# A hybrid mLSTM / RWKV-7 / S5 step: other places for the in-projections computed ahead, and a last stage whose sums are on VectorE

## The chip, the cores and the metric

The kernel runs on one core of a Trainium2 chip. The metric is device time in microseconds. A core has TensorE (PE in the profile; its weight loads stand apart as PEld), VectorE (DVE), ScalarE (ACT), GpSimd (POOL) and SyncE (SP). Each engine works off its own instructions in order. SP computes nothing here: every transfer of this kernel is issued from its one queue, in order.

## What is computed

One layer runs over 520 tokens: 512 of one prompt and 8 samples with states of their own. The width is 1024.

```
x   = LayerNorm(x)
z   = x @ W_in                       # 12424 columns, cut among the parts below
y_A = (mLSTM(xm, ig, fg) gated by og, normed, + skip) * silu(z_A) @ w_bm
y_B = (RWKV-7(r, k, v, decay, a) normed, + bonus)     * silu(z_B) @ w_br
y_C = (S5(u) + D u, GELU, GLU)                        * silu(z_C) @ w_bs
x'  = LayerNorm(ALPHA * x + (sum_b sigmoid(g_b) * y_b) @ w_out)
```

The new states of all three mixers are outputs too. Everything is f32, and so are the weights that are read.

## The kernel before

**In-projections.** The normed input stands transposed in SBUF, cut in two parts `xh` and `xl`. An in-projection of 128 columns (`inproj`, line 142) loads 128 columns of `W_in` in two halves through the three `wraw` buffers (`load_w`, lines 123 to 132). ScalarE copies each half to `whi` (line 130), VectorE subtracts to get `wlo` (line 131); both tiles have two buffers. Then 48 matmuls (`gemm`, line 134) compute hi*hi + hi*lo + lo*hi over eight row tiles, for 256 and for 264 tokens. An output product (`w_br`, `w_bs`, `w_bm`) has the same form with other left and right sides.

**Fills.** In-projections that are needed later are computed ahead, one at a time, and parked in DRAM. They are 44 items of the list `fills` (lines 303 to 316): eight of S5's input u (`fill_u`), then 36 more (`fill_z`), in the order og, z_C, z_A, the gate of branch S5 (eight each), xm (two) and the gate of branch RWKV (two). Each takes a turn of the weight buffers and ends with a store (`zsave` or `ud`). Their pool `fl` stands on the left side and is closed after RWKV (line 362).

**RWKV** (`rwkv`, from line 393) needs 25 in-projections of its own: the small ranks first, then for each of eight column tiles k, r and v. `rcol` (line 421) runs one fill ahead of each. A projection ends with the small copy `shn` on GpSimd (line 354). The column tiles go in four pairs. A pair has its elementwise work, an inverse (62 dependent VectorE operations, lines 595 to 601), and a serial recurrence of eight steps (`chain`, line 633), in which TensorE, ScalarE and VectorE hand over to each other; each step has one copy `rs` on VectorE (line 652). After the last pair the 19 fills that remain are written down in one go (line 796).

**S5, mLSTM and the merge.** S5 (line 945) is interleaved with branch RWKV of the merge, `other(1)`; mLSTM (line 1235) with branch S5 of the merge, which begins with the GLU. `other(0)`, the branch of mLSTM, comes by itself. `out_branch` (line 1562) multiplies by the branch's output matrix, one column tile after another; VectorE gates the result, and for the second and third branch GpSimd adds it to the sum `mg` (line 1588).

**Last stage.** `final` (line 1642) splits `mg`, loads and splits `w_out`, and makes the closing matmuls. The residual needs the input norm's gain and offset: GpSimd multiplies and adds them on five tiles of 1024 columns (line 1682). The saved input `xr` (2 MB) goes into the space of `xh`, and the broadcast rows `xg` into that of `xl`, so that their loads stand behind the last in-projection. The rows `lng` of the last norm go into the space of the gates.

**What sets the order.** The program order is a priority. A planner (Tile, with a simulated timeline) lays each engine's instructions in an order of its own: an instruction goes ahead when its inputs and buffers are there by its reckoning, and what comes first in the program has precedence. So fills that are written down last run between the instructions of the last pair. `issue_after(x)` keeps the instructions of a block that are on the engine of x behind x.

Of the kernel before, what the change touches and what calls it, by code (L numbers as in the profile page):

```python
# [15 lines left out]
P = 128  # L16
D = 1024
# [16 lines left out]

C_XM, C_IG, C_FG, C_OG, C_ZM = 0, 1024, 1028, 1032, 2056
C_RC, C_ZR, C_U, C_ZS, C_GM = 3080, 6280, 7304, 8328, 9352


@with_exitstack
def hybrid_step(ctx: ExitStack, tc: tile.TileContext, I, O):  # L40
# [79 lines left out]
    RB = 3  # L120
    ahead = {}

    def load_w(src, m=P):
        hi = wp.tile([P, KT, P], F32R, tag="whi", bufs=2, name="whi")
        lo = wp.tile([P, KT, P], F32R, tag="wlo", bufs=2, name="wlo")
        src = src.rearrange("(k p) c -> p k c", p=P)
        for k, eng in ((slice(0, KT // 2), weng[0]), (slice(KT // 2, KT), weng[1])):
            raw = wp.tile([P, KT // 2, P], F32, tag="wraw", bufs=RB, name="wraw")
            dma(raw[:, :, 0:m], src[:, k])
            A.activation(hi[:, k, 0:m], raw[:, :, 0:m], AF.Copy)  # L130
            eng.tensor_tensor(lo[:, k, 0:m], raw[:, :, 0:m], hi[:, k, 0:m].bitcast(F32), op=ALU.subtract)  # L131
        return hi, lo
# [135 lines left out]
    flc = ExitStack()  # L268
    fl = flc.enter_context(tc.tile_pool(name="fl", bufs=1))
    zsave, fills = {}, []  # L270

# [31 lines left out]
    for ct in range(KT):  # L303
        fills.append((fill_u, ct))
    for b, c0 in enumerate((C_OG, C_ZS, C_ZM, C_GM + 2 * D)):
        zd = dr.tile([KT, P, N], F32, name=f"zsave{b}")
        for ct in range(KT):
            fills.append((fill_z, (c0 + ct * P, zd[ct])))

    zx = dr.tile([KT, P, N], F32, name="zsave5")  # L310
    for ct in range(2):
        fills.append((fill_z, (C_XM + ct * P, zx[ct])))

    zd = dr.tile([KT, P, N], F32, name="zsave4")
    for ct in range(2):
        fills.append((fill_z, (C_GM + D + ct * P, zd[ct])))

# [43 lines left out]
    rwkv(tc, I, O, env)  # L361
    flc.close()
    mrg = Merge(tc, I, O, env)
    weng[:] = [V, V]
    mrg.open("mr", 1, 4)
    interleave(s5(tc, I, O, env), mrg.other(1), 1.5)
    mrg.pctx.close()
    weng[:] = [V, V]
    mrg.open("ms", 1, 4)
    interleave(mlstm(tc, I, O, env), mrg.s5(), 0.42)  # L370
    mrg.pctx.close()
    mrg.open("mf", 3, 5)
    for _ in mrg.other(0, ahead=True):
# [19 lines left out]
def rwkv(tc, I, O, env):  # L393
# [24 lines left out]
    def rt(name, tag="t", bufs=TB):  # L418
        return rp.tile([P, N], F32, tag=tag, bufs=bufs, name=name)

    def rcol(j):
        rc = rp.tile([P, 1 + N], F32, tag="rc", bufs=1, name="rc")
        e.fill()
        return e.rcol(j, rc, rt("xr"))
# [370 lines left out]
    dma(e.ybsave[:, :, T:N].rearrange("c p b -> p c b"), bvs)  # L795
    e.fill(len(e.fills))
    ctx2.close()
# [147 lines left out]
def s5(tc, I, O, env):  # L945
# [20 lines left out]
    for pi in range(KT // 2):  # L966
# [48 lines left out]
        for j in range(2):  # L1015
# [23 lines left out]
            for h in range(2):  # L1039
                tr(p[:, h * P:(h + 1) * P], kt[:, h])  # L1040
            for h in range(2):
                A.activation(ko[:, j].rearrange("p (m h c) -> p m h c", h=2, c=SC)[:, :, h],
                             p[:, h * P:(h + 1) * P].rearrange("p (m h c) -> p m h c", h=2, c=SC)[:, :, h], AF.Copy)
            gms.append(gm)
            ebs.append(eb)
        kf = ko.rearrange("p j c -> p (j c)")
        V.tensor_tensor(kf[0:SC], kf[0:SC], dm.rearrange("p g c -> p (g c)"), op=ALU.add)
# [461 lines left out]
class Merge:  # L1509
# [52 lines left out]
    def out_branch(self, b, wname, ah, al, permuted=False, gates=None):  # L1562
        e, V, G = self.e, self.tc.nc.vector, self.tc.nc.gpsimd
        mg = self.mg
        for ct in range(KT):
            if gates:
                th = gates[ct]
            else:
                th = self.gate(b, ct, self.t2("gth"))
                yield  # L1570
            hi, lo = e.load_w(self.I[wname][0, :, ct * P:(ct + 1) * P])

            def ev(s, n, p):
# [9 lines left out]
                for dst, g, y in parts:  # L1583
                    if self.first:
                        V.scalar_tensor_tensor(dst, g, 1.0, y, op0=ALU.add, op1=ALU.mult)  # L1585
                    else:
                        V.scalar_tensor_tensor(g, g, 1.0, y, op0=ALU.add, op1=ALU.mult)
                        G.tensor_tensor(dst, dst, g, op=ALU.add)
            e.gemm(hi, lo, ah, al, ev)
# [52 lines left out]
    def final(self):  # L1642

        e, I, O, fp, mg = self.e, self.I, self.O, self.fp, self.mg
        V = self.tc.nc.vector
        dma, split = e.dma, e.split
        mh, ml_ = self.pair("mg")
        for ct in range(KT):
# [3 lines left out]
        lng = fp.tile([P, 2, D], F32, tag="gt", bufs=1, name="lng")  # L1652
        xr = e.xtp.tile([P, 4, D], F32, tag="xh", name="xr")
        xg = e.xtp.tile([P, 3, D], F32, tag="xl", name="xg")
        G = self.tc.nc.gpsimd
        dma(xr, e.xsave[0:T].rearrange("(a p) c -> p a c", p=P))
        dma(xg[0:NB, 2], e.xsave[T:N])
        for j, nm in enumerate(("ln_in_g", "ln_in_b")):
            dma(xg[:, j], I[nm].unsqueeze(0).to_broadcast([P, D]))
        dma(lng[:, 0, :], I["ln_g"].to_broadcast([P, D]))  # L1660
        dma(lng[:, 1, :], I["ln_b"].to_broadcast([P, D]))
        ws = []
# [11 lines left out]
        for hf in range(2):  # L1674
            woh, wol = ws[hf]
            for tt in (4, 0, 1, 2, 3) if hf else (0, 4, 1, 2, 3):
                n = P if tt < 4 else NB
                x = xr[:, tt] if tt < 4 else xg[:, 2]
                if hf == 0:
                    sts[tt] = fp.tile([P, 2, 6], F32, tag="fst", bufs=5, name="fst")  # L1680
                    for j, op in enumerate((ALU.mult, ALU.add)):
                        G.tensor_tensor(x[:n], x[:n], xg[:n, j], op=op)
                p = e.psg.tile([P, 512], F32, tag="g", name="g")
# [60 lines left out]
```

## Time and profile before

| | |
|---|---|
| runs | 1379.88, 1379.0, 1373.04 us; median 1379.0 |
| profiled execution | 1378.35 us |
| its span, first to last instruction | 1376.3 us |
| TensorE busy | 1254.4 us, 91% |
| VectorE busy | 959.2 us, 70% |
| ScalarE busy | 679.5 us, 49% |
| GpSimd busy | 242.8 us, 18% |
| granted clock of TensorE, mean | 0.947 |

The times of the profile are microseconds from the span's start, except where a row says ns. In rows of the profile `L62` is line 62 of the kernel; a tile written and the tiles read stand as out<-in, and `x48` is a count. A busy TensorE is not one at its peak: its matmuls overlap, and the duration shown for one is longer than the time from its start to the next one's. The granted clock is a share of full speed. In the chain of waits each piece is work, or a transfer, on which the next piece waited.

The stages are: entry to about 60 us; the RWKV loop with its 25 projections to 526 us; its exit with the last pair to about 722; S5 with branch RWKV to about 930; mLSTM with branch S5 to about 1250; branch mLSTM and the closing stage to the end.

### The profile page before, as it was taken

To read this page: it belongs to the slowest core of one execution; us is meant where nothing else is said; L and a number is where in the kernel's file an instruction comes from. 1 tells how busy PE (TensorE), PEld (TensorE's weight loads), DVE (VectorE), ACT (ScalarE), POOL (GpSimd) and SP (SyncE) were. 2 spreads that over 40 slices of the span, in tenths; PEclk is the share of its full clock that TensorE was granted. 3 is DMA by queue.
4 is the path that set the end of the run, shared out by engine and by line. 5 is a ranking of instruction groups with operands and counts; after the bars stand their busy time and mean duration, and the time that the engine had idled before them with its cause. 6 is when DMAs were issued, how large, how long until landed. Compare 5 with 4: busy or idle time off the path is not lost.

```text
span 1376.3 us, 27658 instructions
## 1 busy us (share of the span) xinstructions
PE 1254.4 (91%) x10509; PEld 1147.4 (83%) x10509; DVE 959.2 (70%) x2157; ACT 679.5 (49%) x1492; POOL 242.8 (18%) x396
## 2 busy tenths in 40 slices
PE   4969999999998999999985988996999999999887
PEld 4969988889897889999865988996989888899855
DVE  6694594569357834768836998995776775555857
ACT  4547657465746674453222332334765774453220
POOL 1402211123122311105200020000000011104600
PEclk8989999999999999999977999997999999999999
DMA  6333332213121312354518444546676866465331
GB/s 185 95 91 109 91 97 64 74 50 87 52 78 46 89 55 85 96 147 141 160 29 149 110 97 104 130 99 179 208 225 207 275 200 203 138 201 189 92 107 62
DMA packets 246707, 168.49 MB, mean 122 GB/s; under 512 B 54808, under 2 KB 222106, under 8 KB 246302
## 3 DMA queue, kind: packets, MB, share of 16 engines
q1 hardware_dynamic: 246574, 166.72, 43.0%
q8 instruction: 83, 1.36, 0.4%
q14 instruction: 50, 0.41, 0.1%
HBM read 125.18 MB, written 39.20 MB: 119 GB/s over the span
## 4 chain that ended last, share of the span: by engine, by line
PE 35%; DVE 7%; DMA 5%; issue 2%; SPq 2%; ACT 1%; POOL 0%; DVEq 0%; ACTq 0%; POOLq 0%
PE g L62 23%; PE qk L62 2%; PE ys L62 2%; DVE wlo L131 2%; SPq L53 2%; PE s L62 1%; DMA wraw<-in_w_bm_dram 1%; PE nd L62 1%; PE pn L62 1%; PE v L62 1%; DMA cn<-in_state_mlstm_c_dram 1%; PE cn L62 1%; DMA wraw<-in_w_out_dram 1%; DMA br<-in_s_b_im_dram 1%; PE cy L62 1%
## 5 line engine op out<-in xcount | busy, mean ns | idle before, releaser
L62 PE MATMUL g<-xh,whi 128*128 128x264 f32 (+1 forms) x1552 | 461.2, 297 | 37.8 <-DVE th L1541 16.0
L62 PE MATMUL g<-xl,whi 128*128 128x264 f32 (+1 forms) x1552 | 457.1, 295 | 2.1 <-DVE xl L217 2.1
L62 PE MATMUL g<-xh,wlo 128*128 128x264 f32 (+1 forms) x1552 | 454.8, 293 | 0.2 <-DVE wlo L131 0.2
L62 PEld LDWEIGHTS g<-xh,whi 128*128 128x128 f32 x1552 | 304.4, 196 | 48.5 <-DVE th L1541 17.0
L62 PEld LDWEIGHTS g<-xl,whi 128*128 128x128 f32 x1552 | 304.2, 196 | 5.3 <-DVE xl L217 2.3
L62 PEld LDWEIGHTS g<-xh,wlo 128*128 128x128 f32 x1552 | 303.6, 196 | 4.4 <-issue 1.1
L130 ACT ACTIVATE whi<-wraw 128x512 fp32r<-128x512 f32 x258 | 151.2, 625 | 201.0 <-PE g L62 154.3
L131 DVE TENSOR_TENSOR wlo<-wraw,whi 128x512 fp32r<-128x512 f32 x258 | 197.5, 788 | 75.4 <-ACT whi L130 72.9
L661 DVE SCALAR_TENSOR_TENSOR xv<-xv,pc,cy 64x64 f32<-64x64 f32 x112 | 31.3, 279 | 28.1 <-PE cy L62 25.3
L62 PE MATMUL g<-ysh,whi 128*128 128x256 f32 (+1 forms) x128 | 39.1, 312 | 11.5 <-ACT ysh L258 9.1
L564 DVE TENSOR_TENSOR lr<-gg,maskg 64x256 f32<-64x256 f32 x32 | 13.5, 422 | 47.4 <-ACT la L563 47.3
L601 DVE TENSOR_TENSOR xi<-xi,itmp 128x31 f32<-128x31 f32 (+15 forms) x124 | 42.7, 344 | 3.0
L62 PE MATMUL g<-w_bmh,wlo 128*128 128x264 f32 (+1 forms) x128 | 37.4, 293 | 7.8 <-DVE wlo L131 7.6
L599 DVE TENSOR_TENSOR itmp<-lu,xi 128x31 f32<-128x31 f32 (+15 forms) x124 | 42.2, 340 | 2.9
L647 POOL COPY xv<-yv 64x128 f32<-64x128 f32 x64 | 24.7, 388 | 109.1 <-PE cr L62 53.8
L62 PE MATMUL g<-w_brh,whi 128*128 128x256 f32 (+1 forms) x128 | 37.4, 295 | 2.8 <-DVE mg L1585 2.6
L62 PE MATMUL g<-ysl,whi 128*128 128x256 f32 (+1 forms) x128 | 39.7, 311 | 0.0
L62 PE MATMUL g<-ysh,wlo 128*128 128x256 f32 (+1 forms) x128 | 39.3, 307 | 0.0
L568 POOL TENSOR_SCALAR_AFFINE_SELECT ar<-ar 64x512 f32<-64x512 f32 x32 | 21.2, 664 | 94.8 <-ACT ar L567 72.8
L62 PE MATMUL g<-bsl,whi 128*128 128x264 f32 (+1 forms) x128 | 37.8, 297 | 0.0
L62 PE MATMUL g<-bsh,wlo 128*128 128x256 f32 (+1 forms) x128 | 37.6, 295 | 0.0
L62 PEld LDWEIGHTS g<-ysh,whi 128*128 128x128 f32 x128 | 26.3, 209 | 13.4 <-ACT ysh L258 9.4
(582 smaller groups left out, 2980.8 us busy)
## 6 DMA issues: line engine op xcount, KB each, us to landing
wraw<-in_w_in_dram SPq DMA_DIRECT2D x194, 256.0 KB
zsave<-zf SPq DMA_DIRECT2D x36, 260.0 KB
cn<-in_state_mlstm_c_dram SPq DMA_DIRECT2D x32, 256.0 KB
out_dram<-cn SPq DMA_DIRECT2D x32, 256.0 KB
yb<-yssave SPq DMA_DIRECT2D x16, 260.0 KB
zz<-zsave SPq DMA_DIRECT2D x16, 260.0 KB
wraw<-in_w_br_dram SPq DMA_DIRECT2D x16, 256.0 KB
wraw<-in_s_glu_w_dram SPq DMA_DIRECT2D x16, 256.0 KB
```

The source lines that it names most:

```text
L53: nc.sync.dma_start(out, in_)
L62: TE.matmul(out, lhsT, rhs, start=start, stop=stop)
L130: A.activation(hi[:, k, 0:m], raw[:, :, 0:m], AF.Copy)
L131: eng.tensor_tensor(lo[:, k, 0:m], raw[:, :, 0:m], hi[:, k, 0:m].bitcast(F32), op=ALU.subtract)
L564: V.tensor_tensor(lr[hs(pi), pi, u, :], pv[hs(pi), :, 64:128], maskg[hs(pi)].unsqueeze(1).to_broadcast([64, 4, 64]), op=ALU.mult)
L568: G.affine_select(out=z, in_=z, compare_op=ALU.is_ge, fill=0.0, base=-1, pattern=[[0, 4], [1, 2], [1, 64]], channel_multiplier=-1)
L599: V.tensor_tensor(tv, lu[:, s + 1:32, s:s + 1].to_broadcast([P, r, w]), xi[:, s:s + 1, 0:w].to_broadcast([P, r, w]), op=ALU.mult)
L601: V.tensor_tensor(xi[:, s + 1:32, 0:w], xi[:, s + 1:32, 0:w], tv, op=ALU.add)
L647: G.tensor_copy(xv[hs(1 - pi), pi], yv[hs(1 - pi), pi, :, n, :])
L661: V.scalar_tensor_tensor(dst, xv[hs(pi), pi, ci, :], pcs[ci][hs(pi), n:n + 1], psn[hs(pi), ci, :], op0=ALU.mult, op1=ALU.add)
```

## The change

- `PACE`: of the three projections of an RWKV column tile only k and r have a fill ahead of them, so 17 fills stand in the loop instead of 25.
- `LATE`: four fills are not written down at RWKV's end, which gets 23 instead of 19. They come after branch RWKV of the merge, and their TensorE instructions stand behind the last `kt` transposition of S5.
- The list's order: xm and the RWKV gate stand ahead of the S5 gate, so that the four late fills are column tiles 4 to 7 of the S5 gate. The pool of the fills stands on the right side and lives until mLSTM has ended.
- `out_branch` adds on VectorE, in the S5 and in the mLSTM branch.
- In `final` the residual has tiles of its own. Its load stands behind the load of the first `w_bm` tile's second half, the norm rows behind that of the seventh, `lng` behind that of the eighth. The residual's multiplications and additions are on VectorE.

```diff
+LATE = 4
+PACE = (True,) + 4 * (True, True, False, True, True, False)
...
     def load_w(src, m=P):
...
-            dma(raw[:, :, 0:m], src[:, k])
+            wlast[:] = [nc.sync.dma_start(raw[:, :, 0:m], src[:, k]).ins]
...
-    fl = flc.enter_context(tc.tile_pool(name="fl", bufs=1))
-    zsave, fills = {}, []
+    fl = flc.enter_context(tc.tile_pool(name="fl", bufs=1, side="right"))
+    zsave, fills, marks = {}, [], []
...
-    for b, c0 in enumerate((C_OG, C_ZS, C_ZM, C_GM + 2 * D)):
-        zd = dr.tile([KT, P, N], F32, name=f"zsave{b}")
-        for ct in range(KT):
+    def save(c0, k):
+        zd = dr.tile([k, P, N], F32, name=f"zsave{c0}")
+        for ct in range(k):
             fills.append((fill_z, (c0 + ct * P, zd[ct])))
-    zx = dr.tile([KT, P, N], F32, name="zsave5")
-    for ct in range(2):
-        fills.append((fill_z, (C_XM + ct * P, zx[ct])))
-    zd = dr.tile([KT, P, N], F32, name="zsave4")
-    for ct in range(2):
-        fills.append((fill_z, (C_GM + D + ct * P, zd[ct])))
+    for c0, k in ((C_OG, KT), (C_ZS, KT), (C_ZM, KT), (C_XM, 2), (C_GM + D, 2), (C_GM + 2 * D, KT)):
+        save(c0, k)
...
     rwkv(tc, I, O, env)
-    flc.close()
...
+    def beside():
+        yield from mrg.other(1)
+        with tc.issue_after(marks[-1]):
+            fill(len(fills))
+        yield
-    interleave(s5(tc, I, O, env), mrg.other(1), 1.5)
+    interleave(s5(tc, I, O, env), beside(), 1.5)
...
     interleave(mlstm(tc, I, O, env), mrg.s5(), 0.42)
     mrg.pctx.close()
+    flc.close()
...
+    rcols = list(range(24, -1, -1))
     def rcol(j):
         rc = rp.tile([P, 1 + N], F32, tag="rc", bufs=1, name="rc")
-        e.fill()
+        if PACE[rcols.pop()]:
+            e.fill()
...
-    e.fill(len(e.fills))
+    e.fill(len(e.fills) - LATE)
...
             for h in range(2):
-                tr(p[:, h * P:(h + 1) * P], kt[:, h])
+                last = TE.transpose(p[:, h * P:(h + 1) * P], kt[:, h], e.ident)
...
+            e.marks.append(last.ins)
...
     def out_branch(self, b, wname, ah, al, permuted=False, gates=None):
...
+        self.marks = {}
...
             hi, lo = e.load_w(self.I[wname][0, :, ct * P:(ct + 1) * P])
+            self.marks[ct] = e.wlast[0]
...
                         V.scalar_tensor_tensor(g, g, 1.0, y, op0=ALU.add, op1=ALU.mult)
-                        G.tensor_tensor(dst, dst, g, op=ALU.add)
+                        V.tensor_tensor(dst, dst, g, op=ALU.add)
...
     def final(self):
...
+        xr = fp.tile([P, 4, D], F32, tag="xr", bufs=1, name="xr")
+        xs_ = fp.tile([NB, D], F32, tag="xs", bufs=1, name="xs")
+        with self.tc.issue_after(self.marks[0]):
+            dma(xr, e.xsave[0:T].rearrange("(a p) c -> p a c", p=P))
+            dma(xs_, e.xsave[T:N])
...
-        xr = e.xtp.tile([P, 4, D], F32, tag="xh", name="xr")
-        xg = e.xtp.tile([P, 3, D], F32, tag="xl", name="xg")
-        G = self.tc.nc.gpsimd
-        dma(xr, e.xsave[0:T].rearrange("(a p) c -> p a c", p=P))
-        dma(xg[0:NB, 2], e.xsave[T:N])
-        for j, nm in enumerate(("ln_in_g", "ln_in_b")):
-            dma(xg[:, j], I[nm].unsqueeze(0).to_broadcast([P, D]))
-        dma(lng[:, 0, :], I["ln_g"].to_broadcast([P, D]))
-        dma(lng[:, 1, :], I["ln_b"].to_broadcast([P, D]))
+        xg = e.xtp.tile([P, 2, D], F32, tag="xl", name="xg")
+        with self.tc.issue_after(self.marks[KT - 2]):
+            for j, nm in enumerate(("ln_in_g", "ln_in_b")):
+                dma(xg[:, j], I[nm].unsqueeze(0).to_broadcast([P, D]))
+        with self.tc.issue_after(self.marks[KT - 1]):
+            dma(lng[:, 0, :], I["ln_g"].to_broadcast([P, D]))
+            dma(lng[:, 1, :], I["ln_b"].to_broadcast([P, D]))
...
-                x = xr[:, tt] if tt < 4 else xg[:, 2]
+                x = xr[:, tt] if tt < 4 else xs_
...
-                        G.tensor_tensor(x[:n], x[:n], xg[:n, j], op=op)
+                        V.tensor_tensor(x[:n], x[:n], xg[:n, j], op=op)
```

## Rows read from the trace of the kernel before

**Rows 1.** Stage table: us, busy time (and instructions) of each engine, granted clock, DMA share, GB/s.
```profile
126.00:526.00 400.00, 375.03 (x3528) 346.82 (x3526) 254.91 (x578) 255.85 (x594) 85.37 (x178) 0.97 0.26 72
...
690.00:757.00 67.00, 45.56 (x322) 38.71 (x321) 31.46 (x71) 17.18 (x44) 4.82 (x10) 0.71 0.50 88
757.00:929.00 172.00, 163.56 (x1510) 155.54 (x1509) 164.24 (x320) 59.60 (x127) 15.53 (x22) 0.97 0.48 108
929.00:967.00 38.00, 26.05 (x142) 25.19 (x142) 21.13 (x52) 18.94 (x36) 2.14 (x7) 0.69 0.66 184
967.00:1250.00 283.00, 282.36 (x2121) 252.99 (x2120) 193.11 (x514) 171.19 (x357) 26.19 (x45) 1.00 0.66 205
```
**Rows 2.** Chain of waits, 1200 us to the end: start, us, what.
```profile
1204.46 45.92 PE g L62 x383
...
1252.23 11.00 DMA wraw<-in_w_bm_dram
...
1266.33 2.94 DVE wlo L131 x2
...
1272.66 2.86 DVE wlo L131
...
1284.27 5.85 DVE wlo L131
...
1294.76 3.12 DMA wraw<-in_w_out_dram
...
1311.72 54.75 PE g L62 x254
```
**Rows 3.** Groups of VectorE instructions, of three stretches: count, busy us, mean ns, idle before.
```profile
L131 DVE TENSOR_TENSOR wlo<-wraw,whi 128x512 fp32r<-128x512 f32 x81 | 53.3, 687 | 27.8 <-ACT whi L130 26.1 <-PE gg L62 1.4
...
L1084 DVE TENSOR_TENSOR ta<-ta,tb 128x256 f32<-128x256 f32 x16 | 6.7, 418 | 0.2
...
L766 DVE TENSOR_TENSOR S<-S,vk 128x1024 f32<-128x1024 f32 x4 | 4.9, 1217 | 0.2
```
**Rows 4.** Stage table, from r's to v's projection, column tiles 1, 2, 5 and 6.
```profile
141.50:155.40 13.90, 11.36 (x90) 10.86 (x89) 10.35 (x19) 6.19 (x14) 2.94 (x8) 1.00 0.35 100
188.70:201.90 13.20, 11.35 (x93) 10.94 (x92) 12.93 (x26) 5.72 (x14) 3.71 (x7) 1.00 0.37 101
...
377.70:394.40 16.70, 16.58 (x166) 15.09 (x164) 13.04 (x27) 9.41 (x22) 5.00 (x11) 1.00 0.28 80
445.20:465.20 20.00, 17.51 (x134) 15.40 (x133) 17.34 (x39) 12.83 (x31) 10.30 (x16) 1.00 0.30 84
```
**Rows 5.** Timeline, GpSimd's last `shn` copy; SP's first and last of the 19 stores behind it.
```profile
526.12 0.39 POOL L354 COPY shn<-rc 128x9 f32<-128x9 f32 x1 [5.52 <-ACT rc L351]
...
535.35 0.50 SPq L53 DMA_DIRECT2D zsave<-zf  x1
...
685.59 0.49 SPq L53 DMA_DIRECT2D zsave<-zf  x1
```
**Rows 6.** Timeline of VectorE: copies `rs`, one a step, first, fifth, sixth, eighth.
```profile
625.15 0.29 DVE L652 COPY rs<-cr 64x128 f32<-64x128 f32 x1
...
685.57 0.29 DVE L652 COPY rs<-cr 64x128 f32<-64x128 f32 x1 [0.72 <-ACT rs L651]
...
697.89 0.29 DVE L652 COPY rs<-cr 64x128 f32<-64x128 f32 x1 [1.27 <-ACT rs L651]
...
708.68 0.29 DVE L652 COPY rs<-cr 64x128 f32<-64x128 f32 x1 [1.79 <-ACT rs L651]
```
**Rows 7.** Groups of instructions, 1250 to 1312 us.
```profile
L131 DVE TENSOR_TENSOR wlo<-wraw,whi 128x512 fp32r<-128x512 f32 x14 | 32.1, 2326 | 4.3 <-ACT whi L130 4.2
...
L1682 POOL TENSOR_TENSOR xr<-xr,xg 128x1024 f32<-128x1024 f32 x8 | 20.8, 2603 | 0.3 <-DMA xg<-in_ln_in_g_dram 0.3
```
**Rows 8.** Timeline of SP's queue, 1240 to 1252 us: start, us of issuing.
```profile
1244.12 4.73 SPq L53 DMA_DIRECT2D wraw<-in_w_bm_dram  x4
...
1250.75 0.37 SPq L53 DMA_DIRECT2D xr<-xsave  x1
```

More of the change, by code (lines that the diff above doesn't have):

```diff
@@ L121, in hybrid_step @@
     ahead = {}
+    wlast = []
     def load_w(src, m=P):
```

## The prediction

> **What bounds the kernel now.** I read the stage table first, then the chain of waits at the end, then the queues around the moved work. In the stage table the reader is to see which engine leaves no room in a stage, and where the granted clock falls [rows 1]. TensorE fills the RWKV loop and the mLSTM stage (375 of 400 us, 282 of 283), VectorE fills the S5 stage (164 of 172), and two stretches belong to nobody: 690 to 757 us (TensorE 46 of 67 us, clock 0.71) and 929 to 967 us (142 matmuls in 38 us, clock 0.69). The first is the tail of RWKV and the start of S5, the second the S5 exit. A third is in the chain of waits: from 1252 to 1311 us it goes through transfers and VectorE, not through TensorE [rows 2]. 0.5% of 1379 us, about what a measurement of this kernel can tell from no change, is 6.9 us.
>
> Price of an in-projection: 383 matmuls of the same kind back to back took 45.92 us [rows 2], so its 48 matmuls take **5.75 us** of TensorE. It also has two `wlo` subtractions of 0.69 us on VectorE [rows 3], and two weight loads and a store on SP's queue; GpSimd has no part in the fills that move.
>
> **The change, step by step.** *RWKV loop.* Eight fills leave the loop, each the one ahead of a column tile's v projection. What that saves depends on what fills the stretch from r's to v's projection. Of the eight stretches [rows 4] show four, the odd and the even column tiles with the most and the least VectorE. In the odd ones it is busy 74 to 78% and TensorE carries the stretch: 5.75 us each. In the even ones VectorE, which then also works off a pair's inverse, is busy 87 to 98%, and only its 1.38 us is sure to go; TensorE is busy there too, so I take the middle of 1.38 and 5.75, 3.6 us. Sum d = 4 x 5.75 + 4 x 3.6 = **37 us** by which the last projection of RWKV (526.1 us now, [rows 5]) comes earlier. Ends: 8 x 1.38 = 11, and 8 x 8.35 = 67, the spacing of fills at the exit (below), should every stretch shrink by a whole slot.
>
> *RWKV exit.* Now 19 fills are stored between 535.35 and 685.59 us, 8.35 us apart [rows 5]. The last pair's serial recurrence runs under them: its eight steps begin between 625.15 and 708.68; four steps beside fills took 60.4 us, 15.1 each, the next one 12.3, and those without fills 5.4 [rows 6]. With the change 23 fills stand there. Counted from the last projection R the first is stored at R + 9, the last at R + 9 + 22 x 8.35 = R + 193. The recurrence starts at R + 99, so 94 us = 6.2 of its seven step spacings are slow ones; the other 0.8 takes 10 us at the 12.3 of the step in between: R + 203. Before, the eighth step began at R + 183. The stage thus gives back 20 us of d, and ends 37 - 20 = **17 us earlier**. Ends: 11 - 20 = 9 us later, and 67 - 20 = 47 us earlier. S5 begins with loads into RWKV's buffers, so it moves with that end; its start and its VectorE-bound body are left as they are (0).
>
> *S5 exit.* Four fills come here: 4 x 5.75 = 23 us of TensorE, 5.5 us of VectorE, eight loads and four stores (3.1 MB) on the one queue. The 142 matmuls now there are at most 17 us at 0.12 each, so 17 + 23 = 40 us against a stretch of 38: 2 us over. I add 2 because the GLU's weights and the last S5 outputs share the queue with those transfers: **+4 us**. Ends: 0 (holes and the half clock take all) and 23 (all of it ahead of the GLU). Behind them on TensorE wait the GLU and then mLSTM.
>
> *Additions from GpSimd to VectorE.* In the mLSTM stage 24 additions of at most 0.42 us [rows 3]: 10 us in a stage where VectorE is busy 193 of 283 us and TensorE all the time [rows 1]: **0**, and up to 10 if that cover is gone.
>
> *Last stage.* From the last in-projection's end, 1250.38, to the closing matmuls at 1311.72 are 61.3 us for eight products of 5.75 = 46: 15.3 us lost. What is to be seen in the groups of that stretch is `wlo` at 2326 ns instead of 687 while GpSimd does the 2.6 us residual operations [rows 7]: 14 x 1.64 = 23 us of VectorE. The chain goes three times through it (2.94 for two, 2.86, 5.85), and only then do the loads of `w_out` start, at 1294.76 [rows 2]. Without the stretch those four cost 2.8 instead of 11.65 us, so the closing product starts 8.9 us earlier. VectorE takes on 16 x 0.42 + 10 x 1.22 [rows 3] = 19 us, less than the 23 it gets back; the first residual tile's 2.4 us can be late for what empties the first closing product, and I take 1 us off: **-8 us**. Ends -3 and -13 (2 us of the 15.3 kept for the start). The 2 MB residual load moves from 1250.75 to just behind the second `w_bm` load, which is among the four issued from 1244.12 on [rows 8], and the loads after it queue behind it on SP. Now the load behind it and 1 MB more lands 11.0 us late [rows 2]; two thirds of that is 7.3, of which one product (5.75) covers all but 1.6, inside the ends given. The broadcast input-norm rows come later, beside loads of `w_bm` at one pair per 5.75 us, and `lng` still waits for the gates' tile.
>
> Sum against the profiled execution's 1378.35 us (2.05 more than its span, 0.65 under the median): 1378.35 - 17 + 4 + 0 - 8 = 1357.35; with the 0.65, **1358 us**.
>
> [...] In the trace the granted clock is 1.00 in the four r-to-v stretches [rows 4], and 0.71 and 0.69 in the two where TensorE waits most [rows 1]. A stretch without its fill, some 14 us long, lies between them. It is still nearer to the first kind, so I charge nothing; half way to the second, at a clock of 0.86, it would lose 14 x 0.14 = 2 us, 16 us for eight. [...] By the rows the sum is 1358 us; with the 16 us it is 1374.
>
> **The rivals.** *A bigger gain*: each stretch shrinks by a full slot, d = 67: 47 + 8 - 4 = 51, 1328 us. For it: TensorE is busy 94% of the loop [rows 1]. Against: VectorE in the even tiles.
> *The order is not what the text says*: a planner orders the queues, and might pull the eight fills back into the loop. Then d = 0, but only 15 fills stand at the exit, the last at R + 126: 1.8 slow steps, one of 12.3, 4.2 of 5.4, R + 162 instead of R + 183: 21 - 4 + 8 = 25 earlier, 1354. Against: now every fill behind the 25th is stored after the last projection [rows 5].
> *No change*: VectorE and the tile slots hold the loop, d = 16: 4 us later, then +4 and -8: 0, 1379.
> *The loop's clock falls*, as priced above: 1374, also no measurable change. For it: the two slow stretches. Against: all four stretches shown run at full clock.
> *Slower*: the loop does not shrink at all, because r-to-v is held by the chain of the previous pair and not by the fill, so d = 0; the four extra fills at the exit make two more recurrence steps slow: 20 + 4 - 8 = +16, 1395 us. It decides from d below 9 (20 - 9 + 4 - 8 = 7). For it: VectorE at 98% in one stretch. Against: 74 to 78% in the odd ones, where TensorE is at 82 to 99%.
>
> **How the numbers follow.** Forecast 0.55; bigger gain 0.12; other order 0.05; no change 0.10; clock 0.08; slower 0.10. Faster by over 0.5%: 0.72, within: 0.18, slower: 0.10. The range runs from d = 58 (38 + 8 - 4 = 42 earlier, 1337), so that a small part of the bigger gain is left out, to d = 14 (6 + 4 - 8 = 2 later, 1381), so that the slower case is left out: 1337 to 1381. The bounds of the other terms (0 to 23, 0 to 10, -3 to -13) move the sum less than d does and are not stacked on its ends.
>
> **What would show it.** The last `shn` copy near 489 us instead of 526; 23 stores of fills after it, the last near 682; the eighth step's copy near 692; four more stores between 930 and 970 us with the clock there near 1; `wlo` of the last stage back at 0.69 us, no GpSimd there, the first closing matmul some 52 us after the last in-projection instead of 61. I am wrong if the last projection moves by less than 16 us, if the stretch after S5 grows by over 10 us, or if the last stage stays at 61 us because the `w_out` loads alone set it.

## The result, and the profile after

The changed kernel takes 1392.5 us (median of 4 runs, 1391.6 to 1396.8) against 1378.2 for the kernel before on the same chip: a ratio of 1.0121, 95% interval 1.0103 to 1.0139. It is 14 us slower where 20 us less were forecast. The profiled execution took 1391.6 us, its span is 1389.6, 13.3 us more than before.

The table lists five marks of the traces, in us from the span's start: the last projection of RWKV (its `shn` copy), RWKV's end (S5's first load, `pk`), the last `kt` transposition of S5, the last in-projection's last matmul, the first closing matmul (`woh`), and the span's end.

| | last proj. | RWKV's end | last kt | last in-proj. | first closing | end |
|---|---|---|---|---|---|---|
| before | 526.1 | 725.6 | 913.4 | 1250.2 | 1310.5 | 1376.3 |
| after | 517.9 | 733.0 | 919.8 | 1265.5 | 1323.0 | 1389.6 |
| difference | -8.2 | +7.4 | +6.4 | +15.3 | +12.5 | +13.3 |

So the loop gave 8.2 us, the exit of RWKV took 15.6 back, the S5 body 1.0 less, the stretch from S5's last transposition to the last in-projection took 8.9 more, and the last stage gave 2.0 (126.1 to 124.1 us from the last in-projection to the end).

The stage table of the changed kernel, its stretches shifted with the marks (columns as in [rows 1]):

```profile
118.00:518.00 400.00, 357.62 (x3238) 328.51 (x3236) 248.83 (x565) 247.66 (x576) 83.09 (x186) 0.91 0.21 58
697.00:764.00 67.00, 48.67 (x373) 43.35 (x373) 30.91 (x63) 18.54 (x44) 4.34 (x8) 0.87 0.58 114
764.00:936.00 172.00, 168.01 (x1592) 160.62 (x1591) 167.59 (x326) 66.71 (x139) 21.87 (x22) 1.00 0.54 125
936.00:974.00 38.00, 31.04 (x235) 29.72 (x234) 21.60 (x57) 19.35 (x39) 1.60 (x7) 0.89 0.66 184
974.00:1266.00 292.00, 289.29 (x2145) 259.30 (x2145) 197.10 (x536) 171.24 (x357) 9.16 (x21) 0.99 0.65 202
```

The two slow stretches of [rows 1] have their clock back (0.71 to 0.87, 0.69 to 0.89). The loop has lost some: 0.91 where it was 0.97. The same view from r's to v's projection, the four column tiles of [rows 4]:

```profile
138.00:148.10 10.10, 6.89 (x44) 6.69 (x43) 9.04 (x15) 4.14 (x10) 3.03 (x7) 0.83 0.20 52
181.50:192.20 10.70, 6.91 (x45) 6.71 (x44) 10.61 (x22) 4.19 (x10) 2.67 (x7) 0.84 0.20 51
372.60:388.80 16.20, 14.00 (x117) 12.27 (x116) 11.56 (x23) 7.25 (x18) 5.75 (x12) 0.79 0.12 33
439.60:459.30 19.70, 15.56 (x87) 12.70 (x86) 17.92 (x39) 11.71 (x28) 8.66 (x16) 0.74 0.16 45
```

All four ran at 1.00 before. The first two shrank by 3.8 and 2.5 us instead of 5.75 and 3.6; the last two, with 49 and 47 matmuls fewer, by 0.5 and 0.3.

The timeline of the changed kernel: last projection, first and last of the 23 fills at the exit, the recurrence's first, fifth, sixth and eighth step, RWKV's end, and the first and last of the four late fills (as in [rows 5, 6]).

```profile
517.89 0.55 POOL L352 COPY shn<-rc 128x9 f32<-128x9 f32 x1 [4.58 <-ACT rc L349]
...
529.47 0.34 SPq L55 DMA_DIRECT2D zsave<-zf  x1
...
612.39 0.30 DVE L660 COPY rs<-cr 64x128 f32<-64x128 f32 x1 [6.89 <-ACT rs L659]
...
678.65 0.30 DVE L660 COPY rs<-cr 64x128 f32<-64x128 f32 x1
690.48 0.29 DVE L660 COPY rs<-cr 64x128 f32<-64x128 f32 x1 [2.01 <-ACT rs L659]
...
710.00 0.46 SPq L55 DMA_DIRECT2D zsave<-zf  x1
714.88 0.29 DVE L660 COPY rs<-cr 64x128 f32<-64x128 f32 x1 [3.21 <-ACT rs L659]
...
733.03 0.38 SPq L55 DMA_DIRECT2D pk<-pksave  x1
...
928.15 0.43 SPq L55 DMA_DIRECT2D zsave<-zf  x1
...
957.09 0.38 SPq L55 DMA_DIRECT2D zsave<-zf  x1
```

Every step of the recurrence is now a slow one: (714.88 - 612.39) / 7 = 14.6 us, where the last steps before took 5.4. The order is what the text says: 23 fills, then four late ones.

The last stage of the changed kernel, first its groups from 1265 to 1325 us, then the chain of waits:

```profile
L1697 DVE TENSOR_TENSOR xr<-xr,xg 128x1024 f32<-128x1024 f32 x8 | 9.5, 1208 | 3.6 <-DMA xg<-in_ln_in_g_dram 3.6
L134 DVE TENSOR_TENSOR wlo<-wraw,whi 128x512 fp32r<-128x512 f32 x14 | 9.1, 683 | 8.3 <-ACT whi L133 8.3
```

```profile
1261.78 9.70 DMA wraw<-in_w_bm_dram
...
1272.46 17.55 PE g L64 x144
...
1291.98 5.35 DMA xg<-in_ln_in_g_dram
...
1300.76 2.34 DVE xr L1697 x2
...
1304.64 1.14 DVE xr L1697
...
1311.33 1.20 DVE wlo L134 x2
1312.56 4.66 DMA wraw<-in_w_out_dram
...
1319.28 2.98 DMA wraw<-in_w_out_dram
...
1322.96 7.12 PE g L64 x17
```

`wlo` is back at 683 ns from 2326 [rows 7], as forecast. A load of `w_bm` takes 9.70 us behind the 2 MB of `xr`; from 1290 us the chain goes to the late `xg` row, then through the residual's sums, which stand on VectorE ahead of `wlo`. The loads of `w_out` start late again. What TensorE itself waited for in this stage (us in all, times, longest), in the kernel before from 1250 us, in the changed kernel from 1262 us, and the first loads of `w_out` there:

```profile
PE g L62 <- DVE wlo L131: 7.6, 3, 5.6
PE g L62 <- ACT woh L258: 3.0, 1, 3.0
```

```profile
PE g L64 <- ACT woh L261: 5.2, 1, 5.2
PE g L64 <- DVE gt L1598: 2.4, 2, 2.1
PE g L64 <- DVE wlo L134: 1.3, 1, 1.3
PE g L64 <- ACT gt L1568: 0.9, 1, 0.9
```

```profile
1304.67 16.86 SPq L55 DMA_DIRECT2D wraw<-in_w_out_dram  x8
```

The 0.9 us are the wait behind the load of 9.70 us; until 1271 us TensorE still had the first product's matmuls. The 5.2 us are the wait for `w_out`, and the 2.4 and 1.3 us are for VectorE's gating and `wlo`, which stand between the residual's sums. So 10.6 us of waits became 9.8: they have moved, and the first closing matmul comes 57.5 us behind the last in-projection instead of 60.3.

### The profile page after: what moved, and what is told of

The parts are those of the page before. It is cut to its first block, busy times and chain, and to the rows that moved or that the text cites. A ratio compares the mean times of both kernels' runs of the same rounds, so it can differ in the third digit from the quotient of the medians.

```text
span 1389.6 us, 27631 instructions
## 1 busy us (share of the span) xinstructions
PE 1260.7 (91%) x10509; PEld 1151.8 (83%) x10509; DVE 956.8 (69%) x2207; ACT 682.7 (49%) x1492; POOL 184.2 (13%) x346
## 4 chain that ended last, share of the span: by engine, by line
PE 35%; DVE 7%; DMA 6%; ACT 2%; issue 1%; SPq 1%; DVEq 0%; ACTq 0%
PE g L64 23%; PE qk L64 2%; PE ys L64 2%; PE nd L64 1%; PE s L64 1%; PE pn L64 1%; DVE wlo L134 1%; SPq L55 1%; PE cn L64 1%; DMA zz<-zsave 1%; DMA cn<-in_state_mlstm_c_dram 1%; PE v L64 1%; DMA wraw<-in_w_bm_dram 1%; DMA wraw<-in_w_out_dram 1%; DVE xr L1697 1%
## 5 line engine op out<-in xcount | busy, mean ns | idle before, releaser
L64 PE MATMUL g<-xh,whi 128*128 128x264 f32 (+1 forms) x1552 | 467.7, 302 | 40.4 <-ACT xr L350 18.4
L64 PE MATMUL g<-xl,whi 128*128 128x264 f32 (+1 forms) x1552 | 466.3, 301 | 1.9 <-DVE xl L220 1.9
L64 PEld LDWEIGHTS g<-xh,whi 128*128 128x128 f32 x1552 | 310.7, 200 | 49.4 <-ACT xr L350 20.0
L64 PEld LDWEIGHTS g<-xl,whi 128*128 128x128 f32 x1552 | 310.5, 200 | 7.3 <-DVE xl L220 2.2
L64 PEld LDWEIGHTS g<-xh,wlo 128*128 128x128 f32 x1552 | 309.7, 200 | 3.6 <-issue 0.8
L134 DVE TENSOR_TENSOR wlo<-wraw,whi 128x512 fp32r<-128x512 f32 x258 | 177.9, 713 | 76.5 <-ACT whi L133 75.3
L655 POOL COPY xv<-yv 64x128 f32<-64x128 f32 x64 | 24.2, 380 | 122.1 <-PE cy L64 68.6
L64 PE MATMUL g<-w_bmh,whi 128*128 128x264 f32 (+1 forms) x128 | 36.4, 285 | 3.4 <-DVE gt L1598 2.4
L301 ACT COPY zf<-g 128x256 f32<-128x256 f32 (+1 forms) x56 | 20.6, 368 | 34.3 <-issue 18.7
L64 PE MATMUL g<-bsh,wlo 128*128 128x264 f32 (+1 forms) x128 | 36.8, 289 | 0.0
L64 PE MATMUL g<-w_brh,whi 128*128 128x264 f32 (+1 forms) x128 | 36.3, 288 | 0.3 <-DVE mg L1596 0.3
```

Source lines behind the costliest of these rows:

```text
L64: TE.matmul(out, lhsT, rhs, start=start, stop=stop)
L301: A.copy(z[:, s:s + n], p)
L655: G.tensor_copy(xv[hs(1 - pi), pi], yv[hs(1 - pi), pi, :, n, :])
```

## The experiments

**The parts of the change in RWKV.** The thin loop alone on the kernel before (27 fills at the exit; `PACE` and `rcols` as in the change), and the changed kernel with the full loop (15 at the exit, four late):

```
 e1, on the kernel before:
-        e.fill()
+        if PACE[rcols.pop()]:
+            e.fill()
 e2, on the changed kernel:
-PACE = (True,) + 4 * (True, True, False, True, True, False)
+PACE = 25 * (True,)
```

> The kernel before with the thinner RWKV loop alone: 17 in-projections in the loop, 27 at the exit, none late, last stage as before. Theory (the loop is held by a cycle through single buffers from one pair of column tiles to the next, not by the in-projections): last projection near 518 us (8 earlier, as in the changed kernel); fills stored from there 8.2 us apart, the last near 518 + 9 + 26 x 8.2 = 740; all recurrence steps slow, the eighth near 715; RWKV ends 15 to 25 us later than before, S5 exit and last stage as before: about 1398 us. Rival (what is lost lies at the S5 exit and in the last stage alone, the loop and its exit are neutral): 1379 +- 5 us.

Measured: 1404.3 us, ratio 1.0197 (1.0168 to 1.0225). Last projection 519.3. The last fill and RWKV's end in the timeline of e1's SP queue:

```profile
742.20 0.50 SPq L53 DMA_DIRECT2D zsave<-zf  x1
...
749.88 0.50 SPq L53 DMA_DIRECT2D pk<-pksave  x1
```

The thin loop alone costs 24 us at RWKV's end. The rival that finds the loss elsewhere has fallen.

> The changed kernel with all 25 in-projections back in the RWKV loop; 15 remain at the exit, 4 late, last stage as changed. Theory: last projection near 526 us as before; the last of 15 fills stored near 526 + 9 + 14 x 8.2 = 650; two recurrence steps slow instead of four, the eighth step near 686 instead of 708.7, RWKV's end about 22 us earlier than before; S5 exit +9 as in the changed kernel, last stage -2: 1378 - 22 + 9 - 2 = about 1363 us. Rival (RWKV's end is set by its own tail, the sample states, whatever the fills do): end of RWKV as before, 1378 + 9 - 2 = 1385 us.

Measured: 1376.9 us, ratio 1.0007 (0.9986 to 1.0028), between the theory and its rival. RWKV's end at 714.6, 11.0 us earlier and not 22, and 352.1 us from the last `kt` to the last in-projection instead of 336.8 (the profiled execution is 5.7 us over the median; the same stretch takes 349.4 in e12, which has the same stages before its last). From the last projection to RWKV's end it takes 187.0, 199.5, 215.1 and 230.5 us with 15, 19, 23 and 27 fills (e2, before, after, e1): 3.1 to 3.9 us for each fill at the exit. The four late ones cost about what they save.

**How many in-projections the loop holds.** None at all, and eight more than before:

```
 e3 and e5, on the kernel before:
+PACE = 25 * (False,)
+PACE = (1,) + 8 * (1, 1, 2)
...
-        e.fill()
+        e.fill(PACE[rcols.pop()])
```

> The kernel before with no in-projection ahead in the RWKV loop; all 44 at its exit. It is meant to show what the loop costs without them, by the time of the last projection (526.1 us before, 517.9 with 17 fills). Theory (cycle through single buffers): it comes at 470 to 510 us, the pair's period between 115 and 130 us instead of 130 to 134. Rival (TensorE carries the loop): 25 x 5.75 = 144 us earlier, 382 us, a period near 95 us. Both: 44 fills then follow 8.2 us apart (353 us), and the whole is slower than before by over 80 us.

Measured: 1440.6 us; last projection 486.5. The stage table from 118 us to it:

```profile
118.00:486.00 368.00, 293.80 (x2591) 260.17 (x2592) 228.41 (x527) 216.73 (x517) 81.45 (x180) 0.83 0.13 33
```

25 in-projections out of the loop save 39.6 us, 1.6 each, and the clock is 0.83. The time is as the cycle theory expected; the clock in the row is a cause that neither theory had.

> The opposite of the change in the loop: the kernel before with eight in-projections more in the RWKV loop (two ahead of each v projection, 33 in all), 11 at the exit. Theory (an in-projection in the loop costs 1.0 to 1.6 us, because the loop is held by a chain over several engines; at the exit it costs 2.3 to 4.2): last projection 8 to 13 us later (534 to 539), the last of 11 fills stored 91 us behind it (about 628), the recurrence's eighth step near 675 to 690 instead of 708.7, the whole 10 to 30 us faster: about 1358 us. Rival (an in-projection in the loop costs its TensorE time, 5.75 us): last projection near 572, the whole within 8 us of before or slower.

Measured: 1401.4 us, ratio 1.0196 (1.0166 to 1.0227), last projection 576.2. The stage table of e5, 118 to 518 us:

```profile
118.00:518.00 400.00, 379.66 (x3434) 354.70 (x3433) 240.75 (x548) 244.03 (x569) 75.01 (x165) 0.97 0.29 79
```

My theory has fallen, the rival is right upward: eight more cost 50.1 us, 6.3 each, at a clock of 0.97. So 25 stands at a bend. Above it an in-projection costs about its TensorE time (6.3 us, where its 48 matmuls take 5.75 by [rows 2]); below it, taking one out saves 1.0 (25 to 17) to 1.8 us (17 to none, 31.4 us).

**The single buffer of `la`.** In the kernel before, without in-projections in the loop, and in the changed kernel:

```
-        st["la"] = rp.tile([P, 2 * NCH, CH], F32, tag="la", bufs=1, name="la")
+        st["la"] = rp.tile([P, 2 * NCH, CH], F32, tag="la", bufs=2, name="la")
```

> The kernel before with two buffers for the pair's tile la instead of one, so that the next pair's first products need not wait until the inverse of this pair has read it. Theory (the cycle goes through la): the first la copy of a pair is no longer tied to the end of the pair's inverse (it was within 1.2 us of it in three pairs), and the last projection comes 10 to 40 us earlier than 526 us; total -5 to -30 us. Rival (another single buffer, bk or the six t slots, or VectorE's own work is right behind): last projection within 5 us of 526, total within 5 us of before.

> The kernel with no in-projection ahead in the RWKV loop (e3) with two buffers for la. There TensorE is not full (297 of 373 us busy in the loop), so a link through la can show. Theory (the loop without in-projections is held by the cycle: la free, first products of the even tile, odd tile's three projections and products, inverse, la free; 120 us a pair): with la free the pair's period falls below 110 us and the last projection comes well ahead of 486.5 us, near 450. Rival (the chain goes through many hand-overs between engines, and the next single buffer is as late): last projection between 478 and 488 us.

> The changed kernel with two buffers for la. Theory (with 17 in-projections the loop is held by the cycle through la; with 25, where two la buffers brought nothing, by TensorE): last projection 10 to 25 us ahead of the changed kernel's 517.9 us, the whole near 1375 us. Rival (the chain goes through many hand-overs, la is only one of several): last projection between 512 and 522 us, the whole near 1393 us.

Measured: the last projection comes at 529.5 instead of 526.1 in the kernel before (total ratio 1.0079, 1.0055 to 1.0104), at 474.7 instead of 486.5 without in-projections (1438.5 us), at 505.2 instead of 517.9 in the changed kernel (1387.3 us; 1.0084, 1.0057 to 1.0111). With a full loop the second buffer brings nothing, in a thin one some 12 us. e9 lies between what the two theories expected; e10's projection is where its theory had it, its total between the two.

**The clock.** The row of e3 left a second cause. Here TensorE gets matmuls that nobody reads in the eight removed places, and no other engine gets anything: 24 of 256 columns in each (an estimated 2.9 us at full clock, from 383 in 45.92 us [rows 2]), then 48, then 24 of 32 columns.

```
+    def idle(n):
+        ps = psg.tile([P, 512], F32, tag="g", name="dm")
+        for j in range(n):
+            mm(ps[:, 0:256], xh[:, j % KT, 0:P], xh[:, j % KT, 0:256], start=(j == 0), stop=(j == n - 1))
...
         if PACE[rcols.pop()]:
             e.fill()
+        else:
+            e.idle(24)
```

> The changed kernel with 24 matmuls whose result nobody reads in each of the eight places where an in-projection left the loop (2.9 us each at full clock, 23 us in all; no load, no work on another engine). Clock theory (the thinner loop loses its gain to the half clock): the loop's clock comes back above 0.95 and the last projection comes at 500 to 514 us, earlier than the changed kernel's 517.9 although there is more to do. Chain theory (the wait is elsewhere, TensorE idles): 516 to 522 us, whatever the clock. TensorE-work theory (each matmul costs its time): 541 us.

Measured: 1377.0 us, ratio to the kernel before 0.9993 (0.9974 to 1.0012), 15.6 us under the changed kernel. The stage table of e13's loop to its last projection, and that projection in the timeline:

```profile
118.00:504.00 386.00, 361.77 (x3399) 333.99 (x3398) 247.61 (x564) 246.26 (x577) 83.52 (x184) 0.96 0.22 61
```

```profile
503.77 0.20 POOL L352 COPY shn<-rc 128x9 f32<-128x9 f32 x1 [2.58 <-ACT rc L349]
```

With 23 us of matmuls more the last projection comes 14.1 us earlier, at a clock of 0.96 instead of 0.91. This is the clock theory's number; neither of the others allows an earlier end. e17 below has the same loop in the same order: 503.0 us.

> As the run before it with 48 such matmuls in each place, as many as an in-projection has (46 us in all). Clock theory: clock as before the change, last projection between 505 and 526 us. Chain theory: 518 to 524 us. If an in-projection's cost in the loop is its TensorE time alone: 526 us, as before the change; if its loads and its VectorE work count too, less than that.

Measured: last projection 522.9, clock 0.94 from 118 to 518 us, 1394.1 us (ratio 1.0116, 1.0086 to 1.0146). The number lies within all three ranges and the clock is not above e13's 0.96, so this run does not decide between the theories. But 48 unread matmuls cost nearly as much as the in-projections whose place they take: in a full loop an in-projection costs TensorE's time, and at most 0.4 us each (526.1 less 522.9, by eight) is left for its loads and VectorE's share.

> As e13, but the 24 unread matmuls in each place have 32 columns instead of 256, an eighth of the work. Clock theory: they don't hold the clock, which stays near the changed kernel's 0.91 in the loop; last projection between 514 and 522 us. Order theory (the planner's other order made e13 faster, not the clock): the order is mostly e13's, so the last projection comes near e13's 503.8 or earlier, since there is less to do.

Measured: 1389.3 us, ratio 1.0080 (1.0055 to 1.0105). The same two views of e16:

```profile
118.00:518.00 400.00, 375.86 (x3428) 347.48 (x3428) 249.83 (x567) 247.83 (x579) 79.10 (x185) 0.92 0.21 59
```

```profile
515.15 0.46 POOL L352 COPY shn<-rc 128x9 f32<-128x9 f32 x1 [2.90 <-ACT rc L349]
```

As many matmuls in the same places, an eighth of the columns: the clock stays at 0.92 and the gain is gone but for 2.7 us. They are not an eighth of TensorE's time, as the timelines of e13 and e16 show for the 24 at the second place:

```profile
137.66 3.01 PE L64 MATMUL dm<-xh 128*128 128x256 f32 x24
...
137.03 2.88 PE L64 MATMUL dm<-xh 128*128 128x32 f32 x24
```

So the two kernels hold TensorE about equally long, and "less to do" in the expectation is wrong; what differs is the columns, the clock, and the planner's order, which is another one in the changed kernel, in e13 and in e16. Of e13's 14.1 us, 11.4 go with the wide matmuls. An estimate from the stage tables says that the clock can carry them: a stretch times what its clock lacks to 1 is 36 us in the changed kernel (400 at 0.91), 32 in e16 (400 at 0.92) and 15 in e13 (386 at 0.96), so 21 and 4 us less than in the changed kernel, beside the 14.1 and 2.7 us that were gained. That the other order had no part in the 11.4 is not shown. The busy TensorE of e16's row (375.86 us, as many as the 375.03 before) tells nothing of it: the narrow matmuls counted in full (24 in 2.88 us), and at a lower clock a matmul counted as busy for longer (in the changed kernel's first row from r to v 44 in 6.89 us, 0.157 each at a clock of 0.83; before 90 in 11.36, 0.126 at 1.00, [rows 4]).

**The last stage.** The changed last stage alone on the kernel before (25 and 19 fills); the same with the `xg` rows behind the second `w_bm` load and the residual's sums behind the last `wlo`; and with the loads spread:

```
 e7:
-        with self.tc.issue_after(self.marks[KT - 2]):
+        with self.tc.issue_after(self.marks[1]):
             for j, nm in enumerate(("ln_in_g", "ln_in_b")):
...
+                    with self.tc.issue_after(self.sub):
                         for j, op in enumerate((ALU.mult, ALU.add)):
 e11, e15 (marks and what is loaded behind each):
+        for m, t in ((1, 0), (2, 5), (3, 6), (3, 4), (4, 1), (5, 2), (6, 3)):
+            with self.tc.issue_after(self.marks[m]):
+                if t > 4:
+                    dma(xg[:, t - 5], I[("ln_in_g", "ln_in_b")[t - 5]].unsqueeze(0).to_broadcast([P, D]))
...
+                else:
+                    dma(xr[:, t], e.xsave[t * P:(t + 1) * P])
```

> The kernel before with the changed last stage alone (residual in tiles of its own, its sums and those of all branches on VectorE, loads behind the first, seventh and eighth w_bm load). Theory (the stage has a new wait: the residual's sums stand on VectorE ahead of the wlo of the last w_bm tiles, behind the late rows of the input norm): last in-projection to first closing product 57 to 58 us instead of 60.3, the whole 1 to 4 us faster. Rival (the stage does give 8 us, the changed kernel lost it through its S5 exit): 52 us, the whole 7 to 9 us faster.

> As the run before it, with two things undone: the rows of the input norm are loaded behind the second w_bm load instead of the seventh, and the residual's sums stand on VectorE behind the wlo of the last w_bm tile. Theory (the order on VectorE and the late rows cost the stage its gain): last in-projection to first closing product 51 to 54 us, the whole 7 to 10 us faster than before. Rival (the w_out loads themselves set it): 57 us, no difference to the run before it.

Measured: e6 1378.8 us, ratio 1.0021 (1.0003 to 1.0038), 57.6 us from the last in-projection to the first closing matmul; e7 1377.9 us, 1.0014 (0.9997 to 1.0031), 53.5 us. The marks are as both theories had them, the totals are not: neither kernel is faster than the kernel before. The 57.6 are those of the changed kernel: its S5 exit did not spoil its last stage. In e7 the early rows and the order on VectorE together gave 4 us there, and the closing stretch behind took 3.4 more (68.6 against 65.2). The load behind the 2 MB stands as it was, in e7's chain of waits; TensorE waits 1.3 us behind it, and 0.9 in e6:

```profile
1250.39 9.86 DMA wraw<-in_w_bm_dram
...
1261.24 23.30 PE g L64 x192
```

> The kernel before with the changed last stage alone (as e6), but its loads spread: one residual tile or one row of the input norm behind each of the second to seventh w_bm load, instead of 2 MB in one go behind the first and the rows behind the seventh. Theory (two waits ate the stage's gain: the w_bm load behind the 2 MB, 6 to 7 us of TensorE, and the residual's sums held by the late rows and then ahead of wlo and wol on VectorE): last in-projection to first closing product 48 to 52 us instead of 57.6 (e6) and 60.3 (before), the whole 6 to 11 us faster than before. Rival (VectorE's work in that stretch sets it wherever the loads stand): 56 to 58 us, the whole within 3 us of before.

> The changed kernel with the last stage's loads spread as in e11. Theory (the last stage's loss is the place of its loads, whatever stands before it): last in-projection to first closing product 48 to 50 us instead of 57.5, the whole 8 to 11 us faster than the changed kernel, 1382 to 1385 us. Rival (in the changed kernel something else holds it): within 3 us of 1392.

Measured: e11 1369.2 us, ratio 0.9949 (0.9933 to 0.9964), 48.4 us to the first closing matmul and 114.3 to the end (before 60.3 and 126.1); by the runs' ratio the whole is 7 us faster. e15 1386.9 us, 1.0061 (1.0042 to 1.0079), 48.8 us; its median is 5.6 us under the changed kernel's, by the ratios of both to the kernel before it is 8, against 8 to 11 expected. In its trace the last stage is 10 us shorter and the stages before stand 2 to 3 us later. e11's SP queue in the timeline, then its stage table:

```profile
1246.96 0.46 SPq L55 DMA_DIRECT2D xr<-xsave  x1
...
1252.17 0.51 SPq L55 DMA_DIRECT2D xg<-in_ln_in_g_dram  x1
...
1278.19 1.44 SPq L55 DMA_DIRECT2D xr<-xsave  x1
...
1282.41 7.36 SPq L55 DMA_DIRECT2D wraw<-in_w_out_dram  x3
```

```profile
1250.00:1270.00 20.00, 20.00 (x169) 20.00 (x168) 13.54 (x23) 6.04 (x11) 0.00 (x0) 1.00 0.50 162
1270.00:1290.00 20.00, 20.00 (x168) 20.00 (x168) 18.56 (x32) 6.03 (x11) 0.00 (x0) 1.00 0.51 158
```

TensorE does not stop in these 40 us, and `w_out` is loaded from 1282 us on, not from 1304.67 as in the changed kernel. Up to the first closing matmul e11 has one wait of TensorE left, 2.0 us for `w_out`, where e6 has 10.0 and e7 6.6. The expectation's "6 to 7 us of TensorE" for the load behind the 2 MB is wrong: it was 0.9 in e6. What the spread loads took away are the waits behind the late rows and for `w_out`.

**Together.** e8: 33 in the loop and e7's last stage. e12: full loop, 15 at the exit, four late, e11's last stage. e17: the changed kernel with e13's unread matmuls and e11's loads. e18: e17 with two buffers for `la`. Their edits are those shown.

> Both of the above together: eight in-projections more in the RWKV loop, and the last stage with its rows early and its residual sums behind the last wlo. Theory: the two gains are in stages apart and add, about 1350 us. Rival (either gain is taken back by the other stage's new order): no better than the better of the two alone.

> The same last stage in the kernel of e2: all 25 in-projections in the RWKV loop, 15 at the exit, four behind S5. Theory: the last stage gains as in e11, the stages before it stand as in e2 (RWKV's end 11 us earlier than before, the stretch behind S5 up to 15 longer): the whole 6 to 11 us faster than e2's 1376.9, about 1368 us. Rival (the stretch behind S5 and the last stage share the loss): as e2, 1377 us.

> e13 (24 unread matmuls in the place of each in-projection that left the loop) with the last stage's loads spread as in e11. If the two causes are separate, their gains add: 1377.0 less the 5.5 to 10 us that e15 and e11 gave: 1367 to 1372 us, faster than the kernel before. Rival (the stages between take one of them back): 1377 us.

> As e17 with two buffers for la. If la is a link of its own beside the clock: last projection 5 to 12 us ahead of e17's, the whole 1360 to 1367 us. Rival (with the clock up TensorE carries the loop again, as in e4): last projection within 4 us of e17's, the whole within 4 us.

Measured: e8 1397.1 us, 1.0160 (1.0127 to 1.0192): there were no two gains to add. e12 1366.0 us, 0.9933 (0.9911 to 0.9954), and e17 1368.6 us, 0.9927 (0.9902 to 0.9953): both beat both kernels. e18 1381.2 us, 1.0024 (1.0013 to 1.0035): last projection 507.6 against e17's 503.0, and 359.9 us from the last `kt` to the last in-projection against 348.1. With the clock up (0.95 in the loops of both), `la`'s second buffer brings nothing again, as in e4. Why the later stretch is 12 us longer in e18 was not tried.

## Why the prediction was wrong, step by step

The forecast for the profiled execution was 1357.35 us, 34.3 too little. By steps: the loop 28.8 (d 8.2 instead of 37), the exit -4.4 (15.6 given back instead of 20), the S5 body -1.0, the S5 exit 4.9 (8.9 instead of 4), the last stage 6.0 (-2.0 instead of -8). The first sign that it named for being wrong came: the last projection moved by less than 16 us.

**The step that failed is the clock**, where the prediction put: "It is still nearer to the first kind, so I charge nothing". The four stretches shown without their fill fell from 1.00 to 0.74 to 0.84, the loop from 0.97 to 0.91. Keeping the clock up gives back 11 to 14 us of the 28.8 (e13 against e16 and against the changed kernel; the planner's order is not separated from the 11). By the estimate of length times missing clock the loop lacks 36 us after and 12 before (400 at 0.97), so by it the clock took at most 24 of the 28.8, less where TensorE stood still anyway. The 16 us that the prediction worked out for a clock half way down were of that size, and it gave that case a chance of 0.08. The two slow stretches of [rows 1], 0.71 and 0.69, spoke against charging nothing, and these runs agree with them: the loop's granted clock was 0.97 with 25 in-projections in it, 0.91 with 17, 0.83 with none (before, after, e3). The prediction's sum with the 16 us was 1374 and still 18 short, by the rest of d, the S5 exit and the last stage.

**The rest of d** is not settled. No run keeps the clock without the matmuls that keep it: e13's loop, 22.3 us shorter than before, still has 23 us of unread matmuls in it. With the clock up (0.96) d is thus at least 22, and the 37 is neither refuted nor shown. The prediction's working, that TensorE carries the odd tiles, holds for the loop as a whole above the bend: 6.3 us for each one more (e5), 46 us of matmuls for nearly the old time (e14). Below the bend part of the saving became waits: in the thin loop, and only there, `la`'s second buffer gives 12 us (e9, e10). How much of that is the wait itself and how much the clock behind it (0.93 to 505 us instead of 0.92) stays open.

**RWKV exit.** The mechanism was right: the slow recurrence steps go with the fills beside them, 23 make all seven spacings slow. The price was 15.6 us for four fills, not 20: the two steps that turned slow took 24.4 us together instead of 10.8, so 12.2 each and not 15.1. With d at 8.2 the exit outweighs the loop, as the prediction's "slower" rival had it ("It decides from d below 9"). Its time, 1395, was near; its reason, a chain that holds r to v, was at most a part.

**S5 exit.** The order was as forecast, and the clock there rose to 0.89, not to nearly 1. From the last `kt` to the last in-projection it takes 336.8 to 342.7 us in the eight traces without late fills (before, e1, e4 to e8, e11) and 345.7 to 359.9 in the ten with them (after, e2, e10, e12 to e18), means 341.1 and 349.5: 8 us for four fills, inside the ends 0 to 23, and twice the 4 taken. (e3 and e9, whose fills at the exit run on into S5, are left out.) The kernel before has the shortest stretch of its kind.

**Additions on VectorE.** e6, whose mLSTM stretch (339.2) lies among those without late fills (336.8 to 342.7), shows no loss that a trace can tell. As its runs are 0.2% slower than the kernel before although its last stage is shorter, a loss of some us is not ruled out.

**Last stage.** GpSimd as the cause of the slow `wlo` was right (683 ns, with no GpSimd instruction from 1265 to 1325 us). The 1.6 us left over behind the 2 MB held too: the load took 9.70 us, TensorE waited 0.9. What failed is that the input-norm rows were counted as harmless: they came late and held the sums, the sums held `wlo` and the gating (3.7 us of TensorE's waits), and the `w_out` loads behind them started at 1304.67 (5.2 us). So 2 us came instead of 8, under the low end of 3. With the loads spread the same arithmetic gives 11.9 in e11's trace and 7 by its runs, within the forecast's ends of 3 to 13. That the `w_out` loads alone set the stage is refuted by e11.

## What to carry to other kernels

A stage in which TensorE is busy 94% can stand at a bend: what more work costs (6.3 us) does not tell what less work saves (1.0), in part because the thinner stretch can lose its clock (0.97 to 0.91 here). So read the granted clock of the stretch that a change thins out as a term of the sum, and price work at its new place by the traces on both sides: at the exit each fill cost 3 to 4 us, more than the loop gave. When arithmetic moves off an engine, the loads that feed it decide as much: in the traces the same last stage gave 2 us with the rows of the input norm late and the residual in a lump, and 12 with one load behind each weight load (the whole kernel: nothing in e6, 7 us in e11). And a long load in the chain of waits is not yet a wait of the engine that matters: 9.70 us there were 0.9 us of TensorE.

## What the runs showed of the hardware

Work that nobody reads made a kernel faster: with 192 unread matmuls, an estimated 23 us at full clock by [rows 2], the loop's granted clock was 0.96 instead of 0.91 and the changed kernel took 1377.0 us instead of 1392.5 (1.0121 and 0.9993 of the kernel before, each on its own chip); the same number with an eighth of the columns held TensorE about as long (24 in 2.88 us against 3.01), had the clock at 0.92 and the time at 1389.3. VectorE's two-operand subtraction took 683 ns with GpSimd idle (no instruction from 1265 to 1325 us of the changed kernel) and 2326 beside GpSimd's two-operand operations [rows 7].
